# Windowed attention with queries and keys projected feature-major: rotation by partition-shifted copies instead of transposes

## The chip, the cores and the metric

The kernel runs on one core of a Trainium2 chip. The metric is the device time of one execution in microseconds (us). A core has a matrix engine, TensorE (PE in the rows; PEld is its loading of stationary operands), and three elementwise engines: VectorE (DVE), ScalarE (ACT) and GpSimd (POOL). SyncE (SP) and ScalarE issue the transfers of this kernel. A matmul takes a stationary operand and a moving one; "128x512" is an output of 128 partitions by 512 columns. SBUF and PSUM are the on-chip memories; matmuls write PSUM.

## The reference

A trunk of two layers over 512 latent tokens and 256 context tokens, model width 1024. Layer 0 mixes tokens by an mLSTM, layer 1 by windowed attention; a squared-ReLU feed-forward follows each. The change lies in layer 1's attention: 16 query heads, 4 key and value heads, head size 64, four query heads to a key head. Cut to that:

```python
def _apply_rope(x, cos, sin):        # rotate pairs (j, j + dh/2)
    half = x.shape[-1] // 2
    x1, x2 = x[..., :half], x[..., half:]
    return concatenate([x1 * cos - x2 * sin, x1 * sin + x2 * cos], axis=-1)

q, k, v = split(u @ w_in, [16 * 64, 20 * 64])     # latent tokens; the context gives k, v only
lq, lk = _apply_rope(lq, cos, sin), _apply_rope(lk, cos, sin)
# per block of 128 queries: its own, the previous and the next block of keys, and all the context
s = concat(lq @ lk.T, lq @ ck.T) * scale          # masked to |distance| <= 128
p = exp(s - m);  den = sum(p) + exp(sink - m)     # m: the row's maximum, the sink's logit included
o = (p @ v) / den
y = o @ w_out
```

## The kernel before

All products of activations and weights are made from float32 split in two parts, high and low, each rounded to the fast matmul type: `mm3` (L102) issues three matmuls for one product. A weight unit is 512 KB from HBM; `unit` loads it into a `raw` buffer (issued by SP), ACT casts the high part `whi` (L1043) and DVE subtracts to get the low part `wlo` (L1044). The ring holds three raw units and four split ones. A build-time scheduler fixes the order of each engine's queue, so instructions of one engine can stand in another order than the program text; each engine then runs its own queue strictly in that order.

`keys_begin` and `layer1_mix` make the attention. `proj_part` projects with the tokens on the partitions: 128 tokens of the normalised input (`uH`, `uL` for latent, `uC` for context) are stationary, and 256 columns of weights move, so that an output `pj` is 128 tokens by 256 features. There are 384 such matmuls for queries and 288 for keys and values. `kv_out` and `q_out` take them on:

- rotation, in `rope`: two multiplications by DVE from PSUM (L1861 by cosines, L1864 by sines, the swap of halves being a view of the columns), and an addition (L1865, by DVE for the first tiles and by POOL in the blocks);
- the split: ACT casts the high part (L1881 keys, L1899 queries), DVE subtracts (L1882, L1900), into a tile `ksp` or `qsp` that holds high and low side by side;
- four transposes on PE (L1888 keys, L1905 queries) that bring features to the partitions, high part over low part, and a copy from PSUM (L1890 `ks`, L1908 `qs`, by ACT or DVE).

A score (L1933 to L1940) then needs two matmuls for each range of keys, since both parts lie on the contracted partitions. The 16 blocks (key head g, block j of queries) run through a pipeline of hand-written steps, `PAT`: S scores, maximum (DVE, L1946), exponential (ACT, L1953) and scaling by 1/den (POOL, L1964); T transposes of the weights `e` (PE, L1980) and their copy (ACT, L1985); V their product with the values (PE, L1997 and L2003), whose lower half goes to `yb` by ACT (L2005: 64 partitions of PSUM copied to 64 others) and is added into `yT` by DVE (L2008); F one step of filler. Scores run five steps ahead. Fillers are pieces of other matmul work for PE: before, block n has one tile of keys and values for n up to 3 (key heads 2 and 3), one tile of queries up to n = 13, the transposes of the block before, and two pieces of the output projection (`mm<-y`, six pieces in the last two blocks). Score buffers `s` are two, transposed and projected tiles `pt`, `pj` share three, all in PSUM.

## Time and profile before

| | |
|---|---|
| median of 3 runs | 1511.14 us (1510.61 to 1511.97) |
| the profiled execution | 1511.72 us |
| its span in the trace | 1509.9 us |
| PE busy | 1495.0 us, 99% |
| DVE, ACT, POOL busy | 74%, 47%, 18% |
| granted clock of PE | 0.997 of full speed on the mean |

The span is what the trace sees between the first and the last instruction; 1.8 us of the execution lie around it. Matmuls are pipelined: one starts before the one ahead has ended, so a matmul's cost is the distance from its start to the next start, not its duration. The attention of layer 1 lies between about 910 and 1158 us.

### The profile page before, as it was taken

To read this page: it belongs to the slowest core of one execution; us is meant where nothing else is said; L and a number is where in the kernel's file an instruction comes from. 1 tells how busy PE (TensorE), PEld (TensorE's weight loads), DVE (VectorE), ACT (ScalarE), POOL (GpSimd) and SP (SyncE) were. 2 spreads that over 40 slices of the span, in tenths; PEclk is the share of its full clock that TensorE was granted. 3 is DMA by queue.
4 is the path that set the end of the run, shared out by engine and by line. 5 is a ranking of instruction groups with operands and counts; after the bars stand their busy time and mean duration, and the time that the engine had idled before them with its cause. 6 is when DMAs were issued, how large, how long until landed. Compare 5 with 4: busy or idle time off the path is not lost.

```text
span 1509.9 us, 23723 instructions
## 1 busy us (share of the span) xinstructions
PE 1495.0 (99%) x9145; PEld 1333.2 (88%) x9145; DVE 1110.6 (74%) x2039; ACT 716.4 (47%) x1445; POOL 269.0 (18%) x275
## 2 busy tenths in 40 slices
PE   9999999999999999999999999999999999999998
PEld 5888888878889999999999999888777988888886
DVE  4986638497797878787777768676777874867697
ACT  4544333443674242423424345665666655545454
POOL 0112011321203222312223121323333000000000
PEclk9999999999999999999999999999999999999999
DMA  9233313245132334343443422010110533240321
GB/s 375 79 92 123 113 65 123 67 143 157 57 98 70 125 128 152 100 154 132 134 154 98 153 70 78 29 43 29 57 43 29 196 106 118 72 150 20 107 70 56
DMA packets 46631, 157.27 MB, mean 104 GB/s; under 512 B 5135, under 2 KB 7695, under 8 KB 46391
## 3 DMA queue, kind: packets, MB, share of 16 engines
q1 hardware_dynamic: 45344, 154.25, 31.0%
q8 instruction: 72, 1.18, 0.3%
q10 hardware_dynamic: 1175, 1.51, 0.3%
q14 instruction: 40, 0.33, 0.1%
HBM read 153.64 MB, written 2.10 MB: 103 GB/s over the span
## 4 chain that ended last, share of the span: by engine, by line
PE 93%; DVE 3%; ACT 1%; issue 1%; DMA 1%; POOL 0%; POOLq 0%; DVEq 0%; ACTq 0%
PE mm L102 57%; PE p L102 10%; PE pj L102 5%; PE kept L102 3%; PE pt L1980 2%; PE pb L102 2%; PE pc L102 2%; PE av L1997 2%; PE at L999 2%; PE acc L102 1%; PE at L994 1%; PE s L1940 1%; PE at L958 1%; DMA adaw<-ada 1%; PE arow L102 1%
## 5 line engine op out<-in xcount | busy, mean ns | idle before, releaser
L102 PE MATMUL mm<-h,whi 128*128 128x384 f32 x1024 | 262.6, 337 | 0.0
L1044 DVE TENSOR_TENSOR wlo<-raw,whi 128x1024 fp32r<-128x1024 f32 (+2 forms) x152 | 180.3, 1190 | 76.9 <-ACT whi L1043 74.6
L1043 ACT CAST whi<-raw 128x1024 fp32r<-128x1024 f32 (+2 forms) x152 | 151.0, 998 | 150.7 <-PE mm L102 102.7
L102 PE MATMUL mm<-uH,whi 128*128 128x512 f32 (+1 forms) x496 | 189.0, 385 | 0.0
L102 PE MATMUL mm<-uH,wlo 128*128 128x512 f32 (+1 forms) x496 | 186.8, 378 | 0.0
L102 PE MATMUL mm<-uL,whi 128*128 128x512 f32 (+1 forms) x496 | 186.4, 378 | 0.3 <-DVE uL L651 0.3
L102 PEld LDWEIGHTS mm<-h,whi 128*128 128x128 f32 x1024 | 185.5, 188 | 0.4 <-DVE h L1044 0.2
L269 DVE SCALAR_TENSOR_TENSOR adap<-raw,crow 128x1024 bf16<-128x1024 f32 x128 | 161.9, 1265 | 14.5 <-DMA raw<-ada 13.7
L102 PE MATMUL mm<-h,wlo 128*128 128x384 f32 x512 | 172.1, 336 | 0.0
L102 PE MATMUL p<-t,whi 128*128 128x384 f32 x448 | 114.3, 336 | 0.0
L1043 ACT CAST whi<-sum 128x512 fp32r<-128x512 f32 (+1 forms) x42 | 31.8, 760 | 162.2 <-PE mm L102 90.6
L102 PEld LDWEIGHTS mm<-uH,wlo 128*128 128x128 f32 x496 | 93.4, 188 | 17.2 <-issue 0.2
L102 PEld LDWEIGHTS mm<-uL,whi 128*128 128x128 f32 x496 | 93.5, 189 | 16.4 <-DVE uL L651 0.7
L102 PEld LDWEIGHTS mm<-uH,whi 128*128 128x128 f32 x496 | 93.0, 189 | 15.1
L102 PEld LDWEIGHTS mm<-h,wlo 128*128 128x128 f32 x512 | 96.2, 188 | 0.0
L1044 DVE TENSOR_TENSOR wlo<-wb,whi 128x1024 fp32r<-128x1024 f32 x49 | 59.2, 1221 | 36.4 <-ACT whi L1043 36.3
L1044 DVE TENSOR_TENSOR h<-r,h 128x384 fp32r<-128x384 f32 (+2 forms) x100 | 58.7, 590 | 31.2 <-ACT h L1043 30.9
L102 PEld LDWEIGHTS p<-t,whi 128*128 128x128 f32 x448 | 81.2, 188 | 0.0
L1043 ACT CAST whi<-wb 128x1024 fp32r<-128x1024 f32 x49 | 51.5, 1053 | 57.5 <-PE mm L102 47.9
L102 PE MATMUL mm<-uC,whi 128*128 128x256 f32 x416 | 77.8, 287 | 0.3 <-ACT whi L1043 0.3
L1964 POOL TENSOR_SCALAR e<-e,den 128x512 f32<-128x512 f32 (+1 forms) x64 | 51.5, 816 | 139.5 <-DVE den L1962 71.1
L102 PE MATMUL p<-t,wlo 128*128 128x384 f32 x224 | 75.3, 336 | 0.0
(405 smaller groups left out, 3635.6 us busy)
## 6 DMA issues: line engine op xcount, KB each, us to landing
raw<-ada SPq DMA_DIRECT2D x80, 512.0 KB, 3.6
raw<-w SPq DMA_DIRECT2D x64, 512.0 KB, 3.5
raw<-w2a SPq DMA_DIRECT2D x32, 512.0 KB, 3.4
wb<-w2b SPq DMA_DIRECT2D x28, 512.0 KB, 3.6
adaw<-ada SPq DMA_DIRECT2D x16, 512.0 KB, 11.2
raw<-wqk SPq DMA_DIRECT2D x8, 512.0 KB, 4.3
raw<-wv SPq DMA_DIRECT2D x8, 512.0 KB, 3.5
raw<-wo SPq DMA_DIRECT2D x8, 512.0 KB, 3.7
```

Source lines behind the costliest of these rows:

```text
L102: i = self.nc.tensor.matmul(**kw)
L269: self.tc.keep_in_program_order(nc.vector.scalar_tensor_tensor(out=pr, in0=w, scalar=0.5, in1=self.crow[:, v, :], op0=ALU.mult, op1=ALU.mu ...
L958: mm(out=kv[d][64 * h:64 * h + 64, n * VW:(n + 1) * VW], lhsT=kp[:, d, j, 64 * h:64 * h + 64], rhs=v[:, j, h, :], start=True, stop=True)
L994: mm(out=o[hh][:, ob], lhsT=qs[d][HP[hh], j * P:(j + 1) * P], rhs=C[HP[hh], n - 1, d, :], start=not started, stop=False)
L999: mm(out=o[hh][:, i * VW:(i + 1) * VW], lhsT=pw[g, d, hh][:, i, :], rhs=v[:, 3 * g + i, hh, :], start=False, stop=i == 2)
L1043: keep(self.nc.scalar.copy(out=hi, in_=src))
L1044: keep((eng or self.nc.vector).tensor_tensor(out=lo, in0=src, in1=hi.bitcast(F32), op=ALU.subtract))
L1940: mm(out=lat, lhsT=ql, rhs=k1[:, lo * P:hi * P], start=False, stop=True)
L1964: nc.gpsimd.tensor_scalar(out=out[ii][:, :W], in0=out[ii][:, :W], scalar1=den[:, ii:ii + 1], scalar2=1.0, op0=ALU.mult, op1=ALU.mult)
L1980: nc.tensor.transpose(out=pt[:, i * P:(i + 1) * P], in_=ps_[i][:, n * P:(n + 1) * P], identity=self.ident)
L1997: mm(out=o[i * DH:(i + 1) * DH, :], lhsT=v(n + i), rhs=pq[n + i], start=n == 0, stop=n == len(blks) - 2)
```

## The change

Queries and keys are now projected with features on the partitions (`turned`): 128 columns of weights are stationary and tokens move, 512 at a time for latent tokens (`pq` queries, 192 matmuls; `pk` keys, 48) and 256 for the context (48). The transposes L1888 and L1905 and their copies are gone. Values are projected as before (`values`, `pv`, 144 matmuls of 256 columns), apart from the keys, all four value heads at once.

Rotation works on tiles of 128 features (two heads) by 512 tokens. The swap of halves is now between partitions: ACT copies four pieces of 32 partitions from PSUM into a tile `rx`, each to the place of its partner. DVE multiplies PSUM by the cosines into `rt`, and `rx` by the sines; DVE (keys, first queries) or POOL (queries in the blocks) adds. `stack` writes high and low parts straight into `ks` and `qs`: a cast of 64x512 by ACT and a subtraction by DVE for each head, of which one goes to shifted partitions; keys get two arrangements. The tables of cosines and sines are 256 KB each, twice as many bytes. `ks` becomes one tile instead of two, `qs` one tile for four heads' 512 queries with two buffers instead of one for each block with five, and `yb` has buffers of its own.

The blocks' fillers change: value heads of latent blocks 0 and 1 are projected ahead of the scores, of 2 and 3 between the first five score steps; queries of g = 1 to 3 are projected in blocks 0, 1, 2, 3, 7 and 8 (24 matmuls of 512 each); output pieces lie in the others (`outs`).

```diff
-        w = self.begun
-        self.wkv = [w[:2], w[2:]]
+        self.wkv = w = self.begun
         self.kvc = [self.mm.tile([P, 512], F32, name="pj", tag="mm") for _ in range(2)]
-        at = {(1, 4, 0): 0, (1, 4, 2): 1}
-        for pr in range(2):
-            for j, t in zip((4, 5), self.kvc):
-                for i in range(4):
-                    self.proj_part(self.wkv[pr], j, self.rows_of(u), 256, i, t[:, 256 * pr:256 * pr + 256])
-                    if (pr, j, i) in at:
-                        hooks[at[pr, j, i]]()
+        xs = self.xs(u)["C"]
+        for b in range(2):
+            self.turned(self.kvc[0][:, 256 * b:256 * b + 256], w[b], xs, 0, KT)
+        for j, at in ((4, slice(0, 256)), (5, slice(256, 512))):
+            for i in range(4):
+                self.values(self.kvc[1][:, at], j, self.rows_of(u), 2 * i, 2 * i + 2)
+                if j == 4 and i % 2 == 0:
...
-            nc.scalar.dma_start(out=cs.rearrange("p b d -> p (b d)"), in_=a["cst"][:, C_CS:C_CS + 4 * DH])
-            nc.scalar.dma_start(out=sn.rearrange("p b d -> p (b d)"), in_=a["cst"][:, C_SN:C_SN + 4 * DH])
+            self.cs = sw.tile([P, NL], F32, name="cs")
+            self.sn = sw.tile([P, NL], F32, name="sn")
+            nc.scalar.dma_start(out=self.cs, in_=a["cst"][:, C_CS:C_CS + NL])
+            nc.scalar.dma_start(out=self.sn, in_=a["cst"][:, C_SN:C_SN + NL])
...
+            for m in range(2):
+                self.keys_out(m, self.kvc[0][:, m * NCX:(m + 1) * NCX], slice(NL, T))
+
+            def put(j, ps):
+                nc.scalar.copy(out=vst[j], in_=ps.rearrange("p (a h d) -> p a h d", a=2, h=2))
+            for i in range(2):
+                put(4 + i, self.kvc[1][:, 256 * i:256 * i + 256])
+            xl = self.xs(u)["L"]
+            pk = [self.mm.tile([P, 512], F32, name="pk", tag="mm"), self.at.tile([P, 512], F32, name="pk", tag="at")]
             for kt in range(KT):
+                for b in range(2):
+                    self.turned(pk[b], self.wkv[b], xl, kt, kt + 1)
             wq = {0: [self.unit(a["wsq"][0, i]) for i in range(2)]}
+            for m in range(2):
+                self.keys_out(m, self.rope(sw, pk[m], nc.vector), slice(0, NL))
+            for m in range(2):
+                ps = (self.at, self.mm)[m].tile([P, 512], F32, name="pq", tag=("at", "mm")[m])
+                self.turned(ps, wq[0][m], xl, 0, KT)
+                self.queries_out(sw, 0, m, self.rope(sw, ps, nc.vector))
+
+            def v_steps(j, pool, tag):
+                ps = pool.tile([P, 512], F32, name="pv", tag=tag)[:, :256]
+                for i in range(0, KT, 2):
+                    self.values(ps, j, rows, i, i + 2)
+                    if i < KT - 2:
+                        yield
+                put(j, ps)
+                yield
             for j in range(2):
+                for _ in v_steps(j, *((self.mm, "mm"), (self.at, "at"))[j]):
...
-                def q_steps():
...
+                def q_steps(g, b):
+
+                    if b == 0:
                         wq[g] = [self.unit(a["wsq"][g, i]) for i in range(2)]
+                    ps = pt.tile([P, 512], F32, name="pq", tag="pt")
+                    for kt in range(KT):
+                        self.turned(ps, wq[g][b], xl, kt, kt + 1)
+                        if kt < KT - 1:
+                            yield
+                    self.queries_out(sw, g, b, self.rope(sw, ps, nc.gpsimd))
+                    yield
...
+                qat = {0: (1, 0), 1: (1, 1), 2: (2, 0), 3: (2, 1), 7: (3, 0), 8: (3, 1)}
+                outs = {4: 3, 5: 3, 6: 2, 9: 3, 10: 3, 11: 2, 12: 2, 13: 2, 14: 6, 15: 6}
...
                 def filler(n):
-                    fs, late[:] = late[:], []
-                    its = chain(kv_steps(n) if n < 4 else (), q_steps(), out_steps(2 if n < 14 else 6))
-                    for _ in range(2):
-                        next(its, None)
-                        yield
-                    for f in fs[::-1]:
-                        f()
-                        yield
-                    yield from its
+                    return chain(q_steps(*qat[n]) if n in qat else (), out_steps(outs.get(n, 0)))
 
...
-                for _ in range(4):
+                fl = chain(v_steps(2, pt, "pt"), v_steps(3, pt, "pt"))
+                for _ in range(5):
                     next(sg)
-                for _ in q_steps():
-                    pass
-                for f in late[:1]:
-                    late.pop(0)()
-                for _ in range(5 - 4):
-                    next(sg)
+                    next(fl, None)
+                    next(fl, None)
                 for n, (g, j) in enumerate(todo):
...
+    def turned(self, ps, w, xs, i0, i1):
+
+        for kt in range(i0, i1):
+            sl = slice(kt * P, (kt + 1) * P)
+            self.mm3(ps, w[0][:, sl], w[1][:, sl], *xs(kt), kt == 0, kt == KT - 1)
+
+    def values(self, ps, j, rows, i0, i1):
+
+        for kt in range(i0, i1):
+            hi, lo = self.wkv[2 + kt // 4]
+            sl = slice(kt % 4 * 256, kt % 4 * 256 + 256)
+            self.mm3(ps, *rows(kt, j), hi[:, sl], lo[:, sl], kt == 0, kt == KT - 1)
+
...
+    def rope(self, sw, ps, eng):
+        x, t = [sw.tile([P, NL], F32, name=n, tag=n, bufs=2) for n in ("rx", "rt")]
+        nc.vector.tensor_tensor(out=t, in0=ps, in1=self.cs, op=ALU.mult)
+        for i in range(4):
+            o = (i ^ 1) * 32
+            nc.scalar.copy(out=x[o:o + 32], in_=ps[32 * i:32 * i + 32])
+        nc.vector.tensor_tensor(out=x, in0=x, in1=self.sn, op=ALU.mult)
+        eng.tensor_tensor(out=t, in0=t, in1=x, op=ALU.add)
+        return t
+
+    def stack(self, outs, x):
...
+        for e, pair in enumerate(outs):
+            r, o = [slice(64 * i, 64 * i + 64) for i in (e, 1 - e)]
+            for out, hi, lo in zip(pair, (r, o), (o, r)):
+                nc.scalar.copy(out=out[hi], in_=x[r])
+                h = pair[0][r].bitcast(F32)
+                nc.vector.tensor_tensor(out=out[lo], in0=x[r], in1=h, op=ALU.subtract)
...
+    def keys_out(self, m, x, cols):
+        ks = self.swd["ks"]
+        self.stack([[ks[:, i, 2 * m + e, cols] for i in range(2)] for e in range(2)], x)
+    def queries_out(self, sw, g, m, x):
+        if m == 0:
+            self.swd["qs"][g] = sw.tile([P, 4, NL], F32R, name="qs", tag="qs", bufs=2)
+        q = self.swd["qs"][g]
+        self.stack([[q[:, 2 * m + e, :]] for e in range(2)], x)
...
-            yb = sw.tile([DH, 512], F32, name="yb", tag="sp", bufs=4)
+            yb = sw.tile([DH, 512], F32, name="yb", tag="yb", bufs=2)
...
-    c, s = np.cos(ang), np.sin(ang)
+    c, s = np.cos(ang).T, np.sin(ang).T
+    return [np.tile(np.concatenate(t, 0), (2, 1)).astype(np.float32) for t in ((c, c), (-s, s))]
-    o["wskv"] = np.stack([_rhs(np.ascontiguousarray(kv[:, :, pr]).reshape(D, 256), 4) for pr in range(2)])
-    o["wsq"] = np.stack([_rhs(w[:, 256 * g:256 * g + 256], 4) for g in range(KVH)])
+    o["wskv"] = np.concatenate([_mblocks(w[:, 1024:1280]), _rhs(np.ascontiguousarray(w[:, 1280:]), 4)], 0)
+    o["wsq"] = np.stack([_mblocks(w[:, 256 * g:256 * g + 256]) for g in range(KVH)])
```

How this moves instructions, at three pieces of two places.

First, ACT between the keys and the first exponential (`whi` casts of weights, `ksp`, `ks`, `qsp`, `qs` as above). Before:

```order
L1890 COPY ks_9543<-pt 128x4x128
L1881 CAST ksp<-rp_9720 128x2x2x64
L1890 COPY ks_9542<-pt 128x4x128
L1881 CAST ksp<-rp_9729 128x2x2x64
L1890 COPY ks_9542<-pt 128x4x128
L1881 CAST ksp<-rp_9738 128x2x2x64
L1899 CAST qsp<-rp_9771 128x4x64
L1890 COPY ks_9542<-pt 128x4x128
L1908 COPY qs<-pt 128x512
L1899 CAST qsp<-rp_9816 128x4x64
L1953 ACTIVATE e,den<-s,nb 128x512 x2
```

After:

```order
L1043 CAST whi<-raw 128x1024
L1853 COPY rx<-pq 32x512 x2
L1864 CAST ks<-rt 64x512 x4
L1853 COPY rx<-pq 32x512 x2
L1671 COPY vst_9543<-pv 128x256
L1043 CAST whi<-raw 128x1024
L1853 COPY rx<-pq 32x512 x2
L1864 CAST qs<-rt 64x512 x2
L1853 COPY rx<-pq 32x512 x2
L1671 COPY vst_9544<-pv 128x256
L1864 CAST qs<-rt 64x512 x2
L1671 COPY vst_9545<-pv 128x256
```

The copies of transposed keys are gone, and before the first queries (`qs`) there now stand eight copies `rx`, casts of keys and queries from `rt`, and two casts of weights.

Second, the end of block 3 (n = 3) and the beginning of block 4, PE. `av` is the weighted sum of values, `s` a score. Before:

```order
L1997 MATMUL av<-ph,vst_9546 64x512
L1997 MATMUL av<-ph,vst_9547 64x512
L1997 MATMUL av<-ph,vst_9548 64x512
L1997 MATMUL av<-ph,vst_9549 64x512
L102 MATMUL pj<-whi,uH_9023 128x256
L102 MATMUL pj<-wlo,uH_9023 128x256
L102 MATMUL pj<-whi,uL_9024 128x256
L102 MATMUL pj<-whi,uH_9025 128x256
L102 MATMUL pj<-wlo,uH_9025 128x256
L102 MATMUL pj<-whi,uL_9026 128x256
L102 MATMUL pj<-whi,uH_9027 128x256
L102 MATMUL pj<-wlo,uH_9027 128x256
```

After:

```order
L1964 MATMUL av<-ph,vst_9547 64x512
L1964 MATMUL av<-ph,vst_9548 64x512
L1900 MATMUL s<-ks,qs 128x256
L1901 MATMUL s<-ks,qs 128x256
L1902 MATMUL s<-ks,qs 128x384
L1904 LDWEIGHTS idb
L1904 MATMUL s<-msk_9532,idb 128x128
L1906 LDWEIGHTS idb
L1906 MATMUL s<-msk_9537,idb 128x128
L1907 MATMUL s<-ks,qs 128x384
L1900 MATMUL s<-ks,qs 128x256
L1901 MATMUL s<-ks,qs 128x256
```

Before, the product with the values is followed by twelve projections; now two scores follow it at once (the second is cut here), a third stands behind them, and block 3's last queries stand ahead of `av`.

The same place on ACT, from the exponential ahead to the copies `ph` of block 4. Before:

```order
L1953 ACTIVATE e,den<-s,nb 128x640
L1881 CAST ksp<-rp_10631 128x2x2x64
L2005 COPY yb<-av 64x512
L1805 CAST y_10819<-yT_9960 128x512
L1805 CAST y_10823<-yT_9960 128x512
L1985 COPY ph<-pt 128x512
L1899 CAST qsp<-rp_10673 128x4x64
L1985 COPY ph<-pt 128x512
L1043 CAST whi<-raw 128x1024
L1953 ACTIVATE e,den<-s,nb 128x640
L1960 ACTIVATE es<-es 128x2
```

After:

```order
L1920 ACTIVATE e,den<-s,nb 128x640
L1043 CAST whi<-raw 128x1024
L1853 COPY rx<-pq 32x512 x4
L1972 COPY yb<-av 64x512
L1864 CAST qs<-rt 64x512 x2
L1920 ACTIVATE e,den<-s,nb 128x640
L1793 CAST y_10513<-yT_9921 128x512
L1793 CAST y_10517<-yT_9921 128x512
L1927 ACTIVATE es<-es 128x2
L1920 ACTIVATE e,den<-s,nb 128x640
L1952 COPY ph<-pt 128x512 x4
```

Ahead of the second exponential of this place (`e`, `den` from `s`) there now stand the cast of weights, four copies `rx`, `yb` and two casts into `qs`; before, a cast of `ksp`, `yb`, two casts of `y`, and pieces of block 4.

## Rows read from the trace of the kernel before

**Rows 1.** The page: busy time by engine, and the chain that ended last.

```profile
PE 1495.0 (99%) x9145; PEld 1333.2 (88%) x9145; DVE 1110.6 (74%) x2039; ACT 716.4 (47%) x1445; POOL 269.0 (18%) x275
PE 93%; DVE 3%; ACT 1%; issue 1%; DMA 1%; POOL 0%; POOLq 0%; DVEq 0%; ACTq 0%
```

**Rows 2.** Windows of layer 1: length; busy us (instructions) PE, PEld, DVE, ACT, POOL; clock, DMA.

```profile
910.00:935.00 25.00, 24.76 (x201) 24.05 (x200) 21.06 (x36) 12.76 (x29) 2.24 (x7) 1.00 0.18 54
935.00:946.00 11.00, 10.32 (x96) 10.08 (x95) 9.48 (x24) 7.73 (x17) 0.00 (x0) 1.00 0.32 96
946.00:1158.00 212.00, 211.17 (x1497) 170.25 (x1496) 146.82 (x343) 135.95 (x314) 64.68 (x84) 1.00 0.13 41
```

**Rows 3.** Waits of PE, 905 to 1180 us: total us, times, longest.

```profile
PE s L1933 <- ACT qs L1908: 0.7, 1, 0.7
```

**Rows 4.** Timeline of PE in 938 to 941 us: start, duration, instruction.

```profile
938.08 0.28 PE L102 MATMUL pj<-wlo,uH 128*128 128x256 f32 x1
...
940.00 0.28 PE L102 MATMUL pj<-whi,uL 128*128 128x256 f32 x1
940.12 0.46 PE L1888 MATMUL pt<-identr,ksp 128*128 128x128 f32 x4
940.41 0.35 PE L102 MATMUL pj<-whi,uH 128*128 128x256 f32 x1
940.60 0.28 PE L102 MATMUL pj<-wlo,uH 128*128 128x256 f32 x1
```

**Rows 5.** Timeline of PE, eleven 512-wide matmuls of the feed-forward stage.

```profile
1200.02 0.39 PE L102 MATMUL mm<-uH,wlo 128*128 128x512 f32 x1
...
1202.29 0.39 PE L102 MATMUL mm<-uH,whi 128*128 128x512 f32 x1
```

**Rows 6.** Groups by line, 905 to 1180 us, shapes apart: busy, mean ns, idle before.

```profile
L1888 PE MATMUL pt<-identr,ksp 128*128 128x128 f32 x48 | 5.5, 247 | 0.0
L1905 PE MATMUL pt<-identr,qsp 128*128 128x128 f32 x64 | 7.5, 240 | 0.0
L1043 ACT CAST whi<-raw 128x1024 fp32r<-128x1024 f32 x22 | 23.1, 1050 | 2.1 <-PE pj L102 1.5 <-PE mm L102 0.2
L1865 POOL TENSOR_TENSOR rp<-rp,rp 128x256 f32<-128x256 f32 x14 | 10.3, 738 | 23.7 <-DVE rp L1864 21.6 <-PE s L1940 2.1
L302 POOL TENSOR_TENSOR ssL<-ssL,sq 128x512 f32<-128x512 f32 x2 | 3.4, 1723 | 3.7 <-ACT sq L298 3.6
L2005 ACT COPY yb<-av 64x512 f32<-64x512 f32 x16 | 9.4, 585 | 18.4 <-PE av L2003 15.8 <-PE av L1997 2.4
L1806 DVE TENSOR_TENSOR y<-yT,y 128x512 fp32r<-128x512 f32 x6 | 4.2, 699 | 0.0
L1953 ACT ACTIVATE e<-s,nb 128x640 f32<-128x640 f32 x32 | 25.6, 798 | 5.6 <-DVE nb L1948 5.5
```

**Rows 7.** Timeline of ACT: three 512-wide copies in a row.

```profile
937.30 1.56 ACT L1890 CAST ks<-pt 128x512 fp32r<-128x512 f32 x3
```

**Rows 8.** Timeline of PE about the fourth block's end: weighted values, then scores.

```profile
1003.73 1.94 PE L1997 MATMUL av<-ph,vst 128*64 128x512 f32 x8
1005.60 0.39 PE L102 MATMUL pj<-whi,uH 128*128 128x256 f32 x1
...
1007.13 0.28 PE L1933 MATMUL s<-ks,qs 128*128 128x256 f32 x1
...
1007.90 0.28 PE L102 MATMUL pj<-whi,uH 128*128 128x256 f32 x1
```

**Rows 9.** Window of the last 9 us, columns as in Rows 2.

```profile
1500.00:1509.00 9.00, 3.25 (x15) 2.36 (x13) 3.87 (x7) 2.90 (x6) 0.70 (x2) 0.81 0.31 117
```

**Rows 10.** Timeline of POOL: the same scaling of e at two places.

```profile
1117.84 2.40 POOL L1964 TENSOR_SCALAR e<-e,den 128x640 f32<-128x640 f32 x2 [6.70 <-DVE den L1962]
...
1130.55 1.58 POOL L1964 TENSOR_SCALAR e<-e,den 128x640 f32<-128x640 f32 x2 [4.79 <-DVE den L1962]
```

**Rows 11.** DMA issues, 900 to 950 us: KB each, median us from issue to landing.

```profile
cs<-cst ACTq DMA_DIRECT2D x1, 128.0 KB, 2.1
```

More of the change, by code (lines that the diff above doesn't have):

```diff
@@ L1661, in layer1_mix @@
                 msk.append(mk)
-            ks = [sw.tile([P, 2, 2, T], F32R, name=f"ks{pr}") for pr in range(2)]
+            ks = sw.tile([P, 2, KVH, T], F32R, name="ks")
             vst = [self.base.tile([P, 2, 2, DH], F32, name=f"vst{j}", tag=f"hC{j}") for j in range(NCH)]
@@ L1678, in layer1_mix @@
             wq = {0: [self.unit(a["wsq"][0, i]) for i in range(2)]}
-            for f in kvl:
-                f()
-            kvl = [self.kv_out(sw, 0, j, pss[j], nc.vector) for j in range(4)]
-            late = []
-            for j in range(2):
-                ps = self.mm.tile([P, 512], F32, name="pj", tag="mm")[:, :256]
-                for i in range(4):
-                    self.proj_part(wq[0], j, rows, 256, i, ps)
-                late.append(self.q_out(sw, 0, j, ps, nc.vector))
-                for f in kvl[2 * j:2 * j + 2]:
-                    f()
@@ L1894, in q_out @@
-    def q_out(self, sw, g, j, ps, eng):
-        nc = self.nc
-        qs = self.swd["qs"]
-        q = self.rope(sw, j, ps, 4, eng)
-        sp = sw.tile([P, 4, 2, DH], F32R, name="qsp", tag="sp", bufs=4)
-        nc.scalar.copy(out=sp[:, :, 0, :], in_=q)
-        nc.vector.tensor_tensor(out=sp[:, :, 1, :], in0=q, in1=sp[:, :, 0, :].bitcast(F32), op=ALU.subtract)
-        def late():
-            pt = self.ptp.tile([P, 512], F32R, name="pt", tag=self.ptag)
-            for i in range(4):
-                nc.tensor.transpose(out=pt[:, i * P:(i + 1) * P],
-                                    in_=sp[:, i].rearrange("p a d -> p (a d)"), identity=self.identr)
-            qs[g, j] = sw.tile([P, 4, P], F32R, name="qs", tag="qs", bufs=5)
-            nc.any.tensor_copy(out=qs[g, j], in_=pt.rearrange("p (h t) -> p h t", t=P))
-        return late
+    def turned(self, ps, w, xs, i0, i1):
+        for kt in range(i0, i1):
+            sl = slice(kt * P, (kt + 1) * P)
+            self.mm3(ps, w[0][:, sl], w[1][:, sl], *xs(kt), kt == 0, kt == KT - 1)
@@ L1915, in scores @@
         mm = nc.tensor.matmul
-        q4 = d["qs"][g, j]
-        k0, k1 = [d["ks"][g // 2][:, i, g % 2, :] for i in range(2)]
+        q4 = d["qs"][g][:, :, j * P:(j + 1) * P]
+        k0, k1 = [d["ks"][:, i, g, :] for i in range(2)]
         lo, hi = max(0, j - 1), min(4, j + 2)
```

86 lines of the change are left out of this document (7 added, 79 removed).

## The prediction

> **What bounds the kernel now.** I read the page first: PE is busy 99% of the span, and the chain of work that ended last runs 93% of the time through PE [rows 1]. So any PE time taken out is a gain of the same size, unless another engine keeps PE waiting in its place. Then the windows of the stage that changes, 910 to 1158 us: PE is busy for 246.3 of 248 us, at full granted clock, with ACT at 156 us, DVE at 177 us and POOL at 67 us [rows 2]. Nobody but PE is near its limit on the mean, but the head (935 to 946 us) has DVE at 86% and ACT at 70%, and PE's one long wait of the stage, 0.7 us for the first queries' copy, lies there [rows 2, 3]. The reader should see two things: what PE issues decides, and the waits for the chain from a projection to the first score are the place to look at.
>
> **What PE saves.** (1) Transposes: 112 matmuls go (48 and 64, [rows 6]), 28 groups of four. What a group costs is read from starts: from 940.00 to 940.60 us a group lies between two projections, and that stretch holds two distances that would be 0.12 us each, so the group takes 0.60 - 0.24 = 0.36 us [rows 4]; the 0.12 is (940.00 - 938.08)/16 in the same rows. 28 x 0.36 = 10.1 us. (2) Width: 240 matmuls of 512 columns (192 for queries, 48 for latent keys) take the place of 480 of 256. Eleven 512-wide starts in the feed-forward stage are (1202.29 - 1200.02)/10 = 0.227 us apart [rows 5], two 256-wide ones take 0.240, so 240 x 0.013 = 3.1 us. Context keys and all values keep their number and width: nothing. (3) The waits of this stage as it stands: 1.75 us of idle PE in the three windows [rows 2]. An idle stretch starts where the 0.28 us row ended, 0.16 us after the next matmul could have started; with an estimated dozen of them some 2.1 us more, in sum 3.9 us. These go in the sense that I count all waits of the new order below. Sum: 17.1 us, the most that can be had.
>
> **What the other engines pay.** ACT gets, for each 128x512 tile, four copies of 32x512, and casts of 64x512. No row has 32 partitions; the nearest is `yb`, 64x512 to shifted partitions, 585 ns on the mean [rows 6]; 128x512 copies in a row take (1.56 - 0.59)/2 = 0.485 us each with 0.59 for the last, where 0.59 is the duration of the single ones [rows 7]. Half the partitions is as long as all, and shifting costs nothing extra, so I take 0.485 for 32 partitions too; the ends are a quarter of it (time by amount of data) and 0.6 (nothing overlaps). DVE's 128x512 with two inputs take 0.70 us [rows 6]. POOL's addition of 128x512: 0.74 at 256 columns, 1.72 for another addition at 512 [rows 6]; I take 1.4, a little under twice the first, and keep 1.3 and 1.7 as ends. A cast of weights takes 1.05 us, an exponential of 640 columns 0.80 [rows 6]. The larger tables (two loads of 256 KB on ACT's queue where 128 KB landed in 2.1 us [rows 11]) are issued some microseconds ahead of the first rotation; even at twice that time they hide behind the 10.9 us of key matmuls. Bytes of weights are the same.
>
> **New wait 1, the first score.** Time 0 is the end of the latent keys on PE. PE then has 48 query matmuls of 0.227 and 48 value matmuls of 0.120, 16.7 us, and a wait of about 0.4 us, because the query weights' casts need buffers that the keys release last: ready at 17.1. ACT has in its order, before the last cast of the first queries: 8 copies `rx` for keys, 8 casts of latent keys, 8 copies for queries and 4 casts of queries (28 x 0.485 = 13.6), 5 short casts of context keys at an estimated 0.3 and two copies of values (about 2.2), two casts of weights (1.9, since neighbours overlap by 0.1): 17.7 us. The low part follows on DVE (0.70 and two hand-overs, 0.8), and I add 0.8 for the times that ACT waits for a sum of DVE: 19.3. So PE waits 2.2 us. Behind it two smaller ones: 0.4 for a copy of values, and about 0.9 for the first transposes, since the exponentials start later by as much. With the weights' 0.4 the head costs 4.0 us; the ends are 1 (cheap copies) and 7 (0.6 each, and DVE late).
>
> **New wait 2, from block 3 to block 4.** Time 0 is the start of the last query matmul. PE: 0.23, then the product with the values, 1.87 (eight rows in the trace for four instructions), two scores of 0.77 each [rows 8], and at 3.6 a third score that needs the buffer of the first, that is, the first one's exponential done. ACT has queued ahead of that exponential: the weights' cast (0.43 to 1.48), four copies `rx` (DVE's cosine product ends at 1.13; copies 1.4 to 3.45), `yb`, and two casts of queries, which wait for DVE (sines, to 4.2) and POOL (sum, to 5.6): 5.65 to 6.7. The exponential ends at 7.5, PE goes on at 7.55: a wait of 3.9 us. Before, twelve projections stood between the values and the next score and hid such a chain; block 4 has no queries to project. Ends: 2.5 and 5.
>
> **The other places.** The same chain stands in the five other query blocks, but there PE's order has the next tile's matmuls and transposes between the values and the score that waits: 5 to 7 us of work against the same 7.5. I take 0.25 us for each of the five, 1.25. Between blocks 11 and 12, where `y` is split with no filler at hand, 1 us; blocks with few fillers, in sum 1 us. These two are guesses within 0 and 3 by the durations above.
>
> **Sum.** 4.0 + 3.9 + 1.25 + 1 + 1 = 11.15 us of waits against 17.1 saved: 5.95 us less. The profiled execution took 1511.72 us (span 1509.9 and 1.8 around it), which gives 1505.8; the median of the runs lies 0.6 below the profiled one: **1505 us**.
>
> **Two rules weighed.** The same scaling of `e` by POOL takes 1.2 us at one place (2.40 for two) and 0.79 at another [rows 10], so something beside it stretches POOL by half. The Trainium skill, page "SBUF — State Buffer", section "SBUF: two separate sides", says that a DVE instruction with two SBUF inputs and a GpSimd instruction exclude each other for their whole length; the change adds such DVE instructions (`rx` by sines, the subtractions). By that rule POOL's sum would be 2.1 instead of 1.4 in the six query blocks, and the time 1509 instead of 1505 if each block were at its limit; rows 10 agree that POOL can be held, but not by whom.
>
> **Rivals.** *A, the waits stay away.* ACT's copies of 32 partitions are much cheaper than `yb`, or the engines run ahead of the places where I put them. What stays are hand-overs, some 1 us: 1511.1 - 17.1 + 1 = 1495. For it: ACT is busy 63% of the stage and DVE 72% [rows 2]. Against it: order on ACT is fixed, and `yb` costs as much as 128 partitions. *B, the gain is eaten up.* After the last 9 us of the kernel, in which PE works a third of the time, the mean granted clock is 0.81 [rows 9], so idle PE is granted its lower level of 1.2 GHz instead of 2.4 for some of the time: 0.38 of 9 us, 3.4 us. If that also follows the two long waits, PE loses half of 3.4 us twice, 3.4 in sum, and with a POOL held by half in each query block (0.7 x 6 = 4.2) and a little more in the head the time comes to 1509 to 1514. The Trainium skill, page "TensorE: Matmul & The Clock Gate", section "HAM oscillation — how this bites in real kernels", states that PE falls to the lower clock after an idle gap; no gap of the kernel before is long enough to show it outside its ends. *C, slower: ACT's queue becomes the bound in all six query blocks.* If the other five had the wait of block 3, 3.9 us each (their next score also needs an exponential behind the same two casts), waits come to 6 x 3.9 + 4.0 + 2 = 29.4 us, 12.3 more than is saved: 1523. It decides from (17.1 - 6)/6 = 1.85 us a block. For it: the order on ACT is the same in all six. Against it: the fillers between.
>
> **How the numbers follow.** Forecast 0.42 (its own range 1500 to 1508), A 0.15, B 0.24, C 0.19. A change of 0.2%, 3 us, is about what a measurement of this kernel tells from none. Faster: forecast and A, 0.57; same: B, 0.24; slower: C, 0.19. The range must leave out no more than 2 in 10: it reaches down to A, 1495, and up into C to 1518 (about 3.3 us a block), and leaves out the rest of C and a bit of A.
>
> **What will show it.** PE's waits in the stage, by line: the first score (`s` for `qs`) some 2 us, the score of block 4 for `e` some 4 us, and little elsewhere; the mean of the 32x512 copies near 585 ns, that of POOL's 128x512 sum near 1.4 us; no PE rows with `identr` in the attention; 512-wide `pq` starts 0.227 apart. The granted clock must be 1.00 from 910 to 1158 us, or B holds. Wrong would make it: copies of 32 partitions at 0.2 us (A), a wait of more than 1.85 us in blocks 0, 1, 2, 7 and 8 (C), or a projection that PE runs slower when the tokens move.

## The result, and the profile after

The changed kernel takes 1516.8 us (median of 6 runs, 1516.08 to 1518.21), the kernel before 1511.28 us (1510.61 to 1512.31) beside it: the ratio is 1.0037, with an interval of 1.0027 to 1.0048. It is 5.5 us slower (0.4%, clear of the spread of the runs), where 1505 was forecast. The profiled spans are 1516.4 and 1509.9 us.

The page of the changed kernel: busy time by engine, and the engines on the chain that ended last (answers [rows 1]).

```profile
PE 1488.4 (98%) x8792; PEld 1313.4 (87%) x8793; DVE 1114.4 (73%) x2004; ACT 735.9 (49%) x1460; POOL 263.3 (17%) x263
PE 89%; DVE 4%; ACT 4%; issue 1%; POOL 1%; POOLq 0%; DVEq 0%; ACTq 0%
```

PE has 6.6 us less busy time, so the work did go, but the span is 6.5 us longer: PE stands still for what it saved and as much again (a matmul at a lower clock counts as busy). The share of the chain that went from PE to DVE, ACT and POOL says who it waits for. The windows of the stage (columns as in [rows 2]: length; busy of PE, PEld, DVE, ACT, POOL; clock; DMA) show where:

```profile
935.00:946.00 11.00, 11.00 (x54) 9.17 (x53) 9.94 (x17) 9.56 (x19) 0.00 (x0) 1.00 0.32 98
946.00:956.00 10.00, 5.71 (x44) 5.35 (x42) 9.24 (x13) 9.74 (x16) 0.00 (x0) 1.00 0.17 52
956.00:1158.00 202.00, 192.10 (x1140) 143.05 (x1142) 138.05 (x301) 141.47 (x314) 57.92 (x71) 0.97 0.11 37
```

From 946 to 956 us ACT is busy for 9.74 of 10 us, DVE for 9.24, PE for 5.71; and behind it the mean clock is no longer 1.00. PE's waits from 905 to 1190 us (total, times, longest; [rows 3] had one of 0.7):

```profile
PE s L1900 <- ACT e L1920: 6.4, 5, 4.7
PE s L1900 <- DVE qs L1866: 4.8, 1, 4.8
PE mm L102 <- ACT y L1793: 1.5, 1, 1.5
PE pt L1947 <- ACT rx L1853: 1.0, 2, 0.6
```

So both long waits that the prediction named are there, at the places it named: the first score, and block 4's score that needs an exponential. On the timeline of PE (start, duration) the first lies between 951.43 and 956.49, and what follows it runs slowly:

```profile
951.31 0.28 PE L102 MATMUL pv<-wlo,uH 128*128 128x256 f32 x1
951.43 0.28 PE L102 MATMUL pv<-whi,uL 128*128 128x256 f32 x1
956.49 0.55 PE L1900 MATMUL s<-ks,qs 128*128 128x256 f32 x1 [4.77 <-DVE qs L1866]
...
958.49 0.41 PE L102 MATMUL pv<-whi,uL 128*128 128x256 f32 x1
958.71 0.41 PE L102 MATMUL pv<-whi,uH 128*128 128x256 f32 x1
```

Ahead of the wait 256-wide matmuls start 0.12 us apart, behind it 0.22. The windows that follow the two waits give the clock:

```profile
951.60:956.30 4.70, 0.11 (x1) 0.00 (x0) 4.25 (x6) 4.55 (x9) 0.00 (x0) 0.96 0.06 24
956.30:959.50 3.20, 3.02 (x12) 2.68 (x13) 2.11 (x4) 2.08 (x4) 0.00 (x0) 0.50 0.48 164
959.50:962.70 3.20, 3.20 (x17) 3.11 (x16) 2.11 (x3) 0.66 (x2) 0.00 (x0) 0.50 0.00 0
962.70:966.00 3.30, 3.30 (x30) 3.21 (x29) 1.00 (x5) 2.07 (x7) 0.00 (x0) 0.99 0.00 0
...
1027.30:1029.50 2.20, 1.96 (x8) 1.58 (x9) 1.84 (x7) 2.09 (x7) 0.00 (x0) 0.57 0.00 0
1029.50:1031.50 2.00, 2.00 (x11) 1.70 (x10) 0.09 (x1) 0.59 (x1) 1.57 (x2) 0.62 0.00 0
1031.50:1036.00 4.50, 4.50 (x26) 3.79 (x25) 2.55 (x5) 1.94 (x4) 0.00 (x0) 1.00 0.00 0
```

6.4 us at 0.50 of full speed, that is at 1.2 GHz, and 4.2 us at about 0.6. What ACT does ahead of the two waits, from its timeline (a row with x4 is four in a row and their time together; in brackets the idle time before):

```profile
944.22 2.35 ACT L1853 COPY rx<-pk 32x512 f32<-32x512 f32 x4
...
948.75 2.53 ACT L1864 CAST ks<-rt 64x512 fp32r<-64x512 f32 x4
...
955.01 1.25 ACT L1864 CAST qs<-rt 64x512 fp32r<-64x512 f32 x2
...
958.93 1.26 ACT L1864 CAST qs<-rt 64x512 fp32r<-64x512 f32 x2 [1.08 <-DVE rt L1855]
...
1018.97 0.80 ACT L1920 ACTIVATE e<-s,nb 128x640 f32<-128x640 f32 x1 [0.49 <-PE pq L102]
...
1019.75 1.03 ACT L1043 CAST whi<-raw 128x1024 fp32r<-128x1024 f32 x1
1020.81 2.34 ACT L1853 COPY rx<-pq 32x512 f32<-32x512 f32 x4
1023.18 0.58 ACT L1972 COPY yb<-av 64x512 f32<-64x512 f32 x1
1025.32 1.26 ACT L1864 CAST qs<-rt 64x512 fp32r<-64x512 f32 x2 [1.56 <-POOL rt L1855]
1026.60 0.79 ACT L1920 ACTIVATE e<-s,nb 128x640 f32<-128x640 f32 x1
```

Groups by line, 905 to 1180 us (busy, mean ns, idle before), answer the durations of [rows 6]:

```profile
L1853 ACT COPY rx<-pq 32x512 f32<-32x512 f32 x32 | 18.5, 577 | 0.5
L1864 ACT CAST qs<-rt 64x512 fp32r<-64x512 f32 x16 | 9.9, 617 | 5.1 <-POOL rt L1855 3.8 <-DVE rt L1855 1.1
L1855 POOL TENSOR_TENSOR rt<-rt,rx 128x512 f32<-128x512 f32 x6 | 7.7, 1283 | 22.6 <-DVE rx L1854 19.0 <-PE pt L1947 3.5
```

A copy lasts what was forecast, 577 ns. But four take 2.35 us, so their starts are (2.35 - 0.58)/3 = 0.59 us apart and not 0.485 as in [rows 7]; casts are (2.53 - 0.62)/3 = 0.64 apart. They don't overlap. The first score starts at 956.49, behind the first cast of the queries (955.01) and its subtraction; the last two casts of the first queries come later (958.93).

### The profile page after: what moved, and what is told of

Read it like the earlier page. It is cut to its first block, busy times and chain, and to the rows that moved or that the text cites. A ratio compares the mean times of both kernels' runs of the same rounds, so it can differ in the third digit from the quotient of the medians.

```text
span 1516.4 us, 22991 instructions
## 1 busy us (share of the span) xinstructions
PE 1488.4 (98%) x8792; PEld 1313.4 (87%) x8793; DVE 1114.4 (73%) x2004; ACT 735.9 (49%) x1460; POOL 263.3 (17%) x263
## 4 chain that ended last, share of the span: by engine, by line
PE 89%; DVE 4%; ACT 4%; issue 1%; POOL 1%; POOLq 0%; DVEq 0%; ACTq 0%
PE mm L102 56%; PE p L102 10%; PE kept L102 3%; PE pb L102 2%; PE pc L102 2%; PE pt L1947 2%; PE at L999 2%; PE pq L102 1%; PE av L1964 1%; PE acc L102 1%; ACT rx L1853 1%; PE at L994 1%; PE arow L102 1%; PE s L1907 1%; PE at L958 1%
```

## The experiments

The theory after the result: ACT's queue sets both long waits, since its copies and casts don't overlap, and the waits also cost clock. Rivals: the clock costs most of it; DVE's subtraction, which ended the first wait, sets it; shifting between partitions makes the copies slow. The kernel before took 1511.3 to 1511.8 us beside each of the runs, so their times are compared with one another and with 1516.8.

**1. The clock.** Matmuls without use fill the two waits (20 ahead of the first score, 19 at block 4's start), all else being nearly as it was.

```diff
+            wps = self.at.tile([P, 512], F32, name="wps1", tag="at")
+            for _ in range(20):
+                self.tc.keep_in_program_order(nc.tensor.matmul(out=wps, lhsT=wz[:, :P], rhs=wz, start=True, stop=True))
...
+                        if n == 4 and c == 0:
+                            wp2 = pt.tile([P, 512], F32, name="wps2", tag="pt")
+                            for _ in range(19):
```

> The changed kernel with 39 extra 128x512 bf16 matmuls on zeros into tiles that nobody reads, placed on PE inside its two long waits (20 ahead of the first score, 19 between two scores at the start of block 4); they are shorter than the waits (about 0.216 us each, 4.3 and 4.1 us, against 4.8 and 4.7 us). Theory (the two waits cost twice: their length, and the lower clock behind them, 6.2 and 3.7 us at half): the granted clock stays at 1.00 through 951 to 964 and 1022 to 1032 us, the waits themselves keep their ends, and the time falls by 3 to 5 us, from 1516.8 to about 1512 to 1514. Rival (the lower clock is covered, since VectorE and ScalarE are behind anyway at these places): the clock rises and the time stays within 1 us of 1516.8.

Measured: 1515.06 us, 1.0023 [1.0014, 1.0033] of before. The clock is 1.00 from 950 to 966 and from 1012 to 1034 us. Only 1.7 us come back by the medians (3.0 by the traces, from the last key matmul to the last `yT`), of the 3.2 + 1.7 = 4.9 that the two slow stretches seem to cost (half of 6.4, and 4.2 x 0.4). PE's waits show part of the rest:

```profile
PE mm L102 <- ACT y L1802: 2.7, 2, 1.5
...
PE pv L102 <- ACT vst L1671: 0.6, 1, 0.6
```

1.2 us more for `y` and 0.6 for a copy of values: the faster PE meets the same ACT a little later. The gain lies between the theory (3 to 5 us) and the rival (under 1): the clock is a part, and the smaller one.

**2. The wait of block 4.** The queries of (2, 1) are projected half in block 3 and half in block 4, so that projections stand between scores again.

```diff
+                    if n == 3:
+                        self.q21 = q_steps(2, 1)
+                        return islice(self.q21, 4)
+                    if n == 4:
+                        return chain(self.q21, out_steps(3))
```

> The second query tile of key head 2 is spread over two blocks: 12 of its 24 matmuls stay in block 3, 12 go to block 4, which had none, so that PE has filler at the start of block 4 and the rotation's chain lies at block 4's end with output pieces behind it. Theory (one place: no filler beside a chain of casts, copies and POOL's sum that stands ahead of an exponential): the wait of 4.7 us for e at 1022 us goes to under 1 us and the lower clock behind it (about 1.9 us) with it: 1510 to 1511.5. Rival (ScalarE's queue is the bound in all blocks): the wait turns up again at the next block's start, time above 1514.

Measured: 1513.94 us, 1.0016 [1.0007, 1.0025]. The wait of 4.7 is gone and the clock is 1.00 from 1015 to 1035; 1.3 us for the transposes come in its place. 2.9 us gained: just more than the rival allows, and only half of the 5.3 to 6.8 of the theory.

**3. The first wait.** The second arrangement of the keys is made by eight transfers within SBUF on SP's queue, in place of ACT's casts and DVE's subtractions.

```diff
-        self.stack([[ks[:, i, 2 * m + e, cols] for i in range(2)] for e in range(2)], x)
+        self.stack([[ks[:, 0, 2 * m + e, cols]] for e in range(2)], x)
+        for i in range(2):
+            r, o = slice(64 * i, 64 * i + 64), slice(64 - 64 * i, 128 - 64 * i)
+            self.nc.sync.dma_start(out=ks[o, 1, 2 * m:2 * m + 2, cols].bitcast(F32), in_=ks[r, 0, 2 * m:2 * m + 2, cols].bitcast(F32))
```

> The second arrangement of the keys (low over high) is made by eight transfers within the on-chip memory from the first arrangement, instead of 8 casts by ScalarE and 8 subtractions by VectorE (about 4 and 4.5 us). Theory (the first score waits for the sum of work queued on ScalarE and VectorE since the keys): the wait of 4.8 us ahead of the first score goes to about 1 us and the lower clock behind it (3.1 us) vanishes: 1509 to 1511. Rival (the wait is set by the queries' own chain, not by the keys' casts ahead of it, or by the transfers' arrival): the wait stays above 3 us and the time above 1515.

Measured: 1514.05 us, 1.0018 [1.0009, 1.0027]. PE's first wait falls from 4.8 to 2.9, with a new name:

```profile
PE s L1903 <- ACT vst L1671: 2.9, 1, 2.9
```

The first score no longer waits for the queries but for the last copy of values `vst`: the pool that the scores use takes over PSUM that the values were projected into (experiment 7 tests this). The queries themselves are ready sooner: their first subtraction ends 19.0 us after the start of the last key matmul, and 22.4 in the changed kernel. The time, 2.8 us less, lies between theory and rival.

**4. Both** (experiments 2 and 3 together).

> Second arrangement of the keys by transfers, and the query tile spread over blocks 3 and 4, together. Theory (two places with a price each, 2.8 and 2.9 us when taken away alone): 1516.8 - 5.7 = about 1511, the time of the kernel before. Rival (one queue of work on ScalarE behind both, so that what one place gives the other takes): 1513 or more.

Measured: 1510.72 us, 0.9991 [0.9981, 1.0001]. The gains add up: 1516.8 - 2.9 - 2.8 = 1511.1. The wait of 2.9 for `vst` stays.

**5. One copy in place of four, and four without a shift.** Which engine sets the waits, and what the shift costs.

```diff
-        for i in range(4):
-            o = (i ^ 1) * 32
-            nc.scalar.copy(out=x[o:o + 32], in_=ps[32 * i:32 * i + 32])
+        nc.scalar.copy(out=x, in_=ps)
```

```diff
-            nc.scalar.copy(out=x[o:o + 32], in_=ps[32 * i:32 * i + 32])
+            nc.scalar.copy(out=x[32 * i:32 * i + 32], in_=ps[32 * i:32 * i + 32])
```

> One copy of 128x512 by ScalarE takes the place of the four shifted copies of 32x512; this leaves out the rotation's swap of halves. Prices the four pieces: 4 x 0.585 = 2.34 us against about 0.59 a tile, 1.75 less on each of ten tiles. Theory: four tiles lie ahead of the first score, 7 us of ScalarE work less, so the wait ahead of the first score goes to below 1 us (VectorE then sets the rest), the wait at block 4 falls from 4.7 to about 3, the lower clock goes in the head: 1516.8 - 4 - 3 - 1.8 = about 1508. Rival (VectorE, busy 4.25 of the 4.7 us of the head's wait, is the limit there): the head's wait falls by less than 2 us, time 1513 or more.

> The changed kernel, the same order on every engine, with the four pieces of 32 partitions copied to their own partitions instead of their partner's; this leaves out the rotation's swap of halves. Asks why copies of pieces stand 0.585 us apart on ScalarE where copies of 128 partitions stand 0.485 apart. If the shift costs it: four take 0.59 + 3 x 0.485 = 2.05 us instead of 2.34. If it is that neighbours work on different partitions: 2.34 as before, and the time within 1 us of 1516.8.

Measured: one copy 1510.85 us, 0.9996 [0.9987, 1.0006]; four without a shift 1517.26 us (one run). The time with one copy lies between theory and rival. No wait for `qs` is left with it, but this doesn't show that ACT alone sets that wait. The scheduler gave PE another order: 60 matmuls of values stand ahead of the first score in place of 48. The queries came hardly sooner. The rows are windows from 0.23 us after the start of the last key matmul to the end of the first queries' subtraction, first in the changed kernel, then with one copy (columns as in [rows 2]):

```profile
934.21:956.34 22.13, 17.26 (x97) 14.87 (x96) 19.75 (x30) 20.36 (x37) 0.00 (x0) 0.99 0.24 72
```

```profile
933.55:954.46 20.91, 18.76 (x109) 16.37 (x109) 19.72 (x30) 14.86 (x27) 0.00 (x0) 1.00 0.26 76
```

ACT has 5.5 us less to do, DVE as much as before, 19.7 us, and the stretch shrinks by 1.2 us. So in the changed kernel ACT's queue is the tighter of two, by about that much; with ACT relieved, DVE's sets the time. The rival, less than 2 us, was right here, though its time (1513 or more) was not. Experiment 3, which relieves both engines, brought 3.4 us. At block 4, too, the queries' casts come only 0.3 us sooner, 6.25 us after the start of the last query matmul (1011.82) in place of 6.53, and ACT waits there for POOL's sum, which waited for DVE:

```profile
1018.07 1.26 ACT L1862 CAST qs<-rt 64x512 fp32r<-64x512 f32 x2 [2.21 <-POOL rt L1853]
```

What remains of waits stands at the values and at `y`, the wait of 4.2 at block 4's start:

```profile
PE mm L102 <- ACT y L1793: 5.7, 2, 4.2
PE pv L102 <- ACT vst L1671: 1.9, 1, 1.9
```

From 905 to 1165 us PE's idle time is 10.9 us in place of 14.6, and behind the wait of 1.9 us the clock stayed at 1.00, which is worth up to 3.2 us: these two account for the 6 us gained.

Without a shift, four copies take as long as with it, in the same order; the shift is free:

```profile
943.96 2.35 ACT L1853 COPY rx<-pk 32x512 f32<-32x512 f32 x4
```

**6. Two tries on what was left of the head**, on top of 4. First the copies `vst` go to DVE (`nc.vector.tensor_copy`). Then the swap, too, is made by transfers:

```diff
+        nc.scalar.copy(out=y, in_=ps)
-            nc.scalar.copy(out=x[o:o + 32], in_=ps[32 * i:32 * i + 32])
+            nc.sync.dma_start(out=x[o:o + 32], in_=y[32 * i:32 * i + 32])
```

> As the run with both, and the copies of the values from PSUM by VectorE instead of ScalarE (six of 128x256): with the keys by transfers the first score waited 2.9 us for such a copy, which stands at the end of ScalarE's queue. Theory: that wait goes to about 1 us and the lower clock with it: 1508 to 1509.5. Rival (queries' casts are late by the same amount): 1511.

> As the run with three, and the swap by transfers: ScalarE copies a 128x512 tile once, four transfers of 32x512 in on-chip memory bring the pieces to their partners. Theory (ScalarE's work in the stage is what the waits come from; one copy for four alone gave 6 us): 1505 to 1508. Rival (a rotated tile comes some 3 us later, and weights wait on SyncE's queue behind transfers that wait for copies): 1510 or more, with waits for whi and qs.

Measured: 1511.19 us, 0.9997 [0.9988, 1.0007], no gain over 4, as the rival had it. The wait has another name and nearly its size:

```profile
PE s L1908 <- ACT rx L1858: 2.5, 1, 2.5
```

With the swap by transfers 1514.54 us, 1.0018 [1.0008, 1.0027]: ACT is idle for more than half of the head now, but the sixteen transfers of 64 KB take 2.0 us each to land, and the first score comes at 963.1 us. The rival's time (1510 or more) came.

**7. PSUM, and the carried pieces**, on top of 4. Both tiles of first queries and the values of blocks 0 and 1 are projected into the pool `at`, so that the scores' pool takes over what is free early. Then the pieces of the output projection that a block leaves are carried on, and one of block 10's three is kept for block 12.

```diff
-                ps = (self.at, self.mm)[m].tile([P, 512], F32, name="pq", tag=("at", "mm")[m])
+                ps = self.at.tile([P, 512], F32, name="pq", tag="at")
-                for _ in v_steps(j, *((self.mm, "mm"), (self.at, "at"))[j]):
+                for _ in v_steps(j, self.at, "at"):
...
-                        parts = self.out_part(g - 1, ys, pt, "pt")
+                        parts += self.out_part(g - 1, ys, pt, "pt")
```

> As the run with transfers and spread tile (1510.7), with other PSUM buffers for the first queries and values, so that the first score's buffer lies where the context's keys and values were, which are copied out early. In that run the first score waited 2.9 us for the last copy of values, whose bank it takes over, though its queries were there. Theory (a bank taken over, not data): the first score's wait falls to under 1.5 us, and with it the lower clock behind it: 1508 to 1509.5. Rival (the second score, whose queries are cast last on ScalarE, then waits instead): 1510 to 1511.

> As the run before, and one piece of the output projection is carried from block 10 to block 12, so that block 12 starts with work for PE while the finished heads' sum is split for the next pieces (a wait of 1.6 us at that place in the changed kernel). Theory: 1.6 us less than the run with the other buffers alone. Rival (work moved, not gained: a like wait at another block's start): within 0.5 us of it.

Measured: 1508.92 us, 0.9984 [0.9975, 0.9993], and 1508.07 us, 0.9978 [0.9969, 0.9987]. Both are faster than the kernel before, by 0.2%, the second 8.7 us faster than the changed kernel. The other buffers did what their theory said: the first score now waits 0.5 us, for the queries. The carried piece brought 0.9 us, between theory (1.6) and rival (0.5), and the two intervals overlap. In the second, the wait for `y` is no longer listed, and the longest are

```profile
PE s L1908 <- ACT e L1928: 1.9, 5, 0.5
PE pt L1955 <- DVE hL L1832: 1.3, 1, 1.3
```

The clock is 1.00 from 910 to 1158 us, with PE busy for 241.6 us of these 248 (233.4 in the changed kernel).

**8. Why the copies don't overlap.** First four whole copies in place of four quarters (`nc.scalar.copy(out=x, in_=ps)` four times):

> Four copies of the whole 128x512 tile take the place of the four of 32x512: as many instructions of as many columns on ScalarE, but each begins at partition 0; this leaves out the rotation's swap of halves. Theory (a copy that begins at another group of 32 partitions than its neighbour can't overlap it): four in a row take 0.59 + 3 x 0.485 = about 2.05 us instead of 2.34. Rival (a chain into one tile, or four in a row as such): 2.34. The order on the engines is not the same, so the time tells little: within 3 us of 1516.8.

Measured: 0.61 us apart, which spoke against start partitions. But all four write the same place, and the program makes each wait for the one before on ACT's own semaphore; so this run tells nothing. (1509.49 us, one run, with another order.) Then copies that write four columns of one buffer, in several forms and with no such wait:

```diff
+        kind = "AACCBDFBDF"[self.nrope]
+            o = {"A": 0, "B": 32 * i, "C": 0, "D": 0, "F": 32 * i}[kind]
+            r = {"A": 0, "B": 32 * i, "C": 0, "D": 32 * i, "F": 0}[kind]
+            nc.scalar.copy(out=y[o:o + h, i], in_=ps[r:r + h])
```

> The four ScalarE copies of a rotation take their source and write their target in other forms, all four of one tile with no wait between them; none swaps halves (the sines multiply the projection itself; the swap is left out). The targets are four columns of one buffer, so no two copies write the same place (with four whole copies into one place, the program made each copy wait for the one before it, so that run says nothing on start partitions). Keys: 32x512, from partitions 0 to 31 to partitions 0 to 31. First queries: 128x512 whole. Query tiles of the blocks, in order of time: first and fourth, 32x512 from another quarter of the partitions each to that same quarter; second and fifth, from another quarter each, always to partitions 0 to 31; third and sixth, always from partitions 0 to 31, to another quarter each. Read is the time that four in a row take. Theory 1, a ScalarE instruction does not start before the end of the one ahead when its source or target begins at another quarter: keys and whole copies 3 x 0.485 + 0.58 = 2.04, the blocks 2.34. Theory 1a, only the source counts: third and sixth 2.04 too. Theory 1b, only the target: second and fifth 2.04. Theory 2, copies of one PSUM tile do not overlap: 2.34 in all. Theory 3, a copy of few partitions does not overlap: 2.34 for all of 32 partitions, keys too, 2.04 for whole ones. The time of the kernel is not the question.

Measured, on ACT's timeline (keys; whole; then the second, third and fourth tile of the blocks; the first is split by other work, the fifth takes 2.35 and the sixth 2.33):

```profile
947.02 2.01 ACT L1858 COPY ry<-pk 32x512 f32<-32x512 f32 x4 [2.33 <-DVE rt L1850]
...
955.27 2.05 ACT L1858 COPY ry<-pq 128x512 f32<-128x512 f32 x4 [1.69 <-DVE rt L1850]
...
998.32 2.35 ACT L1858 COPY ry<-pq 32x512 f32<-32x512 f32 x4
...
1011.38 2.34 ACT L1858 COPY ry<-pq 32x512 f32<-32x512 f32 x4
...
1024.42 2.34 ACT L1858 COPY ry<-pq 32x512 f32<-32x512 f32 x4
```

Theory 1, to 0.03 us. 32 partitions overlap like 128 as long as all start at the same quarter; a source or a target that starts at another quarter, either alone, takes the overlap away, 0.11 us for each instruction. (The kernel took 1522.89 us; why is not shown.) The casts of `rt` fit this by their distances (0.64 apart, 0.62 long); no run varies them.

Copies that overlap here all start at partition 0, so the run alone can't tell a change of quarter from any start but 0. Two neighbours of the changed kernel can, if the casts stand in the order of the program text: both write from partition 64 on, the first out of PSUM from partition 64, the second out of SBUF from partition 0, and they overlap by 0.09 us.

```profile
941.76 0.37 ACT L1864 CAST ks<-pj 64x256 fp32r<-64x256 f32 x1
942.04 1.25 ACT L1864 CAST ks<-rt 64x512 fp32r<-64x512 f32 x2
```

So, by these two, it is the change that counts, and a source in the other memory does not count as one.

## Why the prediction was wrong, point by point

**What PE saves** was right in its distances (its sum is taken up below). No `identr` rows are left in the attention, and 512-wide projections start 0.227 us apart, here from 1015.97 to 1016.65:

```profile
1015.97 0.39 PE L102 MATMUL pq<-uH,wlo 128*128 128x512 f32 x1
...
1016.65 0.39 PE L102 MATMUL pq<-uH,wlo 128*128 128x512 f32 x1
```

**What the other engines pay**, and with it the first score, is the step that failed. The duration was right ("half the partitions is as long as all", 577 ns), as was POOL's sum (1.28 for 1.4) and DVE's products (0.69). But "128x512 copies in a row take 0.485 us each ..., so I take 0.485 for 32 partitions too" took the overlap over from [rows 7], where all copies start at partition 0. Here neighbours start at different quarters (experiment 8): copies stand 0.59 us apart and casts 0.64.

The first score was forecast 19.3 us after the end of the keys and came 956.49 - 934.21 = 22.3 after it; the wait of 2.2 us measured 4.8. The sum's largest term hides the error, since two mistakes cancel. It goes to the last cast of the first queries, 28 pieces, 13.6 us. But the first score waits only for the first of these casts, behind six copies of queries and not eight (the order printed under "The change" has them so). That makes 23 pieces, 14 copies and 9 casts, and these took 13.7 us, four of them starting before the end of the one ahead; at 0.485 each they would have been 11.2. The three missing microseconds stand in the other terms: three casts of weights and the end of a fourth where two were counted (3.6 us for 1.9), seven short casts of context keys where five were counted, with one copy of values (3.1 for 2.2), and ACT's waits for DVE (1.2 for 0.8).

The sum also had no queue of DVE's own, only 0.8 us for ACT's waits and 0.8 behind. DVE has 19.7 us of work up to that score, and with ACT relieved the queries were still not ready before 20.9 us after the keys (experiment 5). So overlapping copies alone would not have given the 19.3. The end of 0.6 us each, which the prediction kept for the range, was the right one for the copies. The 0.4 for values and 0.9 for transposes that were added behind it did not come as waits of their own, so the head's sum, 4.0, was exceeded by about one microsecond only; that is luck in part.

**Block 3 to block 4**: forecast 3.9, measured 4.7. The chain is the one described: weights' cast, four copies (2.34 for an expected 2.05), `yb`, two casts that wait for POOL (1.26 for 1.05), the exponential. PE went on 8.75 us after the start of the last query matmul (1018.79), for 7.55; 0.5 of the difference are these overlaps. Another 0.5 is an exponential that stood ahead of the weights' cast, which the prediction's time 0 left out: the cast began at 0.96 in place of 0.43.

Of the two rules weighed, that DVE and POOL exclude each other shows in this place, but DVE pays. While POOL's sum runs from 1024.03 to 1025.29, a DVE instruction with two inputs in SBUF and one column, which takes 0.15 us at 1027.58, ends with it after 0.63. So it is in four of the six query blocks (0.59 to 0.67 us); POOL's six sums took 1.26 to 1.30 us and not 2.1.

```profile
1024.03 1.26 POOL L1855 TENSOR_TENSOR rt<-rt,rx 128x512 f32<-128x512 f32 x1 [3.55 <-DVE rx L1854]
```

```profile
1024.67 0.63 DVE L1915 SCALAR_TENSOR_TENSOR nb<-mx,nsink 128x1 f32<-128x1 f32 x1
```

**The other places** held on the whole: behind the five other query tiles waits of 1.0, none, none, 0.3 and 0.7 us, for 0.25 each, and 1.5 for `y` between blocks 11 and 12, for 1. Rival C, 3.9 us in each, did not happen, though the time came out on its side.

**The clock** was the second step that failed, a term put at nothing without a reason. "The granted clock must be 1.00 from 910 to 1158 us, or B holds": it was 0.50 for 6.4 us and about 0.6 for 4.2. Rival B had the mechanism and a good size (3.4 us, for the 1.7 to 3.0 that experiment 1 gave back), yet the likeliest case counted it at nothing although it had two waits of its own of 2.2 and 3.9 us. The rule of the Trainium skill that stood beside it (page "TensorE: Matmul & The Clock Gate", section "HAM oscillation — how this bites in real kernels": an idle gap drops PE to the lower clock) agrees with the two waits of 4.7 us.

**The sum.** The waits of the stage come to some 16 us, for 11.15; the slow stretches add 4.9 at their face; 16.7 were saved with before's own waits as they show in its trace (3.5 for 3.9). That makes 16 + 4.9 - 16.7 = 4.2 slower; the traces differ by 6.3 at the end of the attention (last `yT` 1163.9 against 1157.6 us). About 2 us I could not place. They lie in PE's busy time rather than in waits: from 905 us to the last `yT` it falls from 250.9 to 244.3 us, and with 4.9 of slow clock taken off that is some 11.5 us less, where transposes and width were to save 13.2. The range, up to 1518, held the time, but as part of C.

## What to carry to other kernels

An engine that is busy half of the time can still set the end, where a chain passes through its queue in a fixed order: add up what stands in the queue ahead of the very link that is waited for, with the distances between starts of just such neighbours, not of the same size elsewhere. Do it for each engine of the chain: here DVE's queue was only some microsecond shorter than ACT's, so relieving ACT alone brought little. And where an experiment makes a wait vanish, look when the data came, since another order can hide the same lateness. Ask of each long wait that a plan accepts what the matmul clock does behind it. And when a wait is taken away, read the next name in the list before counting the gain: here `qs`, `vst` and `rx` stood one behind the other, and only with the third change did the kernel become faster than before.

## What the runs showed of the hardware

- ScalarE overlaps neighbouring instructions by some 0.1 us (0.48 us apart at 0.58 long) only if source and target start at the same quarter of the partitions as those of the one ahead. Two casts shown in experiment 8 suggest that a source counts only against one from the same memory. The Trainium skill, page "VectorE: DVE Perf Modes", section "Two Vector instructions with no wait between them", states such a rule for Vector instructions; experiment 8 shows it for ScalarE's copies.
- A copy from PSUM takes ScalarE 577 ns at 32x512 and 589 at 128x512; a shift between partitions changes nothing.
- A DVE instruction with two inputs in SBUF that met POOL's sum ended with it, 0.59 to 0.67 us long for 0.15.
- Waits of 1.5 us, and of 1.9 in experiment 5, left the clock at 1.00, waits of 4.7 brought 0.50 and 0.6, and one of 2.5 us in the first kernel of experiment 6 was followed by 5.5 us at 0.76 and 0.63. After one of 2.9 us it stayed at 1.00 in experiment 3 and fell to 0.73 and 0.66 for 5.6 us in experiment 4, with the same wait: what decides there stays open. The rows:

```profile
955.00:958.00 3.00, 2.79 (x23) 2.71 (x24) 2.25 (x4) 1.67 (x4) 0.00 (x0) 1.00 0.16 64
```

```profile
955.40:958.20 2.80, 2.66 (x16) 2.62 (x17) 2.05 (x4) 1.59 (x4) 0.00 (x0) 0.73 0.17 67
958.20:961.00 2.80, 2.80 (x19) 2.71 (x18) 1.62 (x2) 0.00 (x0) 0.00 (x0) 0.66 0.00 0
```
